# A two-block transformer step: the second block's linear-attention stage put in another order

## Chip, cores and metric

One core of a Trainium2 chip runs the kernel. The metric is device time in microseconds for one execution, lower is better. TensorE (PE) does the matrix products, VectorE (DVE), ScalarE (ACT) and GpSimd (POOL) the element work, SyncE (SP) issues the loads.

## What is computed

256 tokens of width 1024 go through two blocks. The first (windowed attention, latent attention, a large expert lookup) ends with a norm and isn't touched. The second projects the normed tokens to linear-attention queries, keys, values and gates, and to queries, keys and values of a banded attention; both outputs go through one output projection, then a gated feed-forward follows. Cut to what the change touches:

```python
qkv = silu(causal_depthwise_conv(concat([gq, gk, gv]), conv_w))    # 12 tiles of 128 features
q_g, k_g = l2_norm(heads(gq)), l2_norm(heads(gk));  v_g = heads(gv)
beta = sigmoid(gb);  g = -exp(a_log) * softplus(ga + dt_bias)
# per head and chunk of 64 tokens:
G = cumsum(g);  decay = exp(G[:, None] - G[None, :]) where causal
A = (k * beta) @ k.T * decay, strictly lower
u, w = solve(A + I, [v * beta, k * beta * exp(G)])                 # the inverse
qk = q @ k.T * decay, causal
# over the four chunks in turn:
v_new = u - w @ S;  o = (q * exp(G)) @ S + qk @ v_new
S = S * exp(G[-1]) + (k * exp(G[-1] - G)).T @ v_new
o_g = rms_norm(o) * silu(heads(gz))
o_s = sliding_window_attention(rms_norm(sq), rms_norm(sk), sv, sinks)
x = x + gate1 * (concat([o_g, o_s]) @ w_out)
```

## The kernel before

Everything is in `tile_kernel`. A tile framework schedules it: the order in the program text is a priority, an instruction that is ready may go ahead of one that isn't, and each engine then runs its list in the fixed order so found. `issue_after` holds an instruction behind another on its engine.

Large products are made in three passes of reduced-width operands: `Split` (L95, L96) cuts a weight tile into a high part (ScalarE) and a low part (VectorE, or GpSimd for a share `share["pool"]` of them), and `mm3` (L115 to L117) or `features` (L123 to L125) issue high times high and the two mixed products. Small products and transposes are plain float32. `ring` says how many raw and split buffers the weights rotate through.

PSUM has eight banks: four tagged `acc` (`ps_acc`), two `mm` (`ps_mm`), two `tr` (`ps_tr`). The 256 tokens are two blocks b of 128, each of two chunks of 64.

The second block's middle runs as follows. `conv(n)`, n = 0 to 11, makes 128 features of queries (0 to 3), keys (4 to 7) or values (8 to 11): 24 products of 256 columns, two copies on ScalarE, three multiply-adds on VectorE (L1021), a silu (L1022) into `F`. Keys go first; `to_tokens` transposes them, `head_rstd` takes their norm (a power on GpSimd, L142), `kn` is the normed key and `kF` its transpose. Values, then queries follow. Then the decays (L1080 to L1126): cumulated gates, their exponentials `eG`, `eK`, `dec`, `DT`, products with `beta` (`bDT`, `first1`), and on GpSimd `gt`, `bt`, `kbe`, `kd` and `zs`.

`inverse(b, pool)` is a generator: it inverts the triangular matrix in five doubling factors n = 2 to 32, each of a transpose of T (L1186), a copy by ScalarE (L1188), products with A (L1192), a masked copy by VectorE (L1195), products with the transpose (L1199), and a subtraction (L1203). It ends with `wT` and `u`. `recur(b)` walks the two chunks of a block with state `Sb`. `heads` norms the banded attention's queries and keys, `window` makes its scores, softmax (exponentials L1340, division on GpSimd L1347), transposes and product with the values (L1361). `window_heads` is the first half of the output projection, for the banded attention's output `oT`; it needs both blocks.

What order they are in is written at the end: block 0's inverse starts within the query projection `project(0, 512, prq)`, then goes on beside `heads`; block 1's runs beside block 0's recurrence and the rest of `heads` and `window`; block 1's recurrence runs beside `window_heads`. The core lines:

```python
aside = chain(heads(), window())
first = inverse(0, b2)
for k, _ in enumerate(project(0, 512, prq)):
    if k in (3, 6):
        next(first)
...
together(first, (next(aside, None) for _ in range(ASTEPS)))
r0 = recur(0)
together(inverse(1, dr), r0, aside)
...
together(chain(r0, recur(1)), window_heads())
```

`together` takes one step of each generator in turn.

Of the kernel before, what the change touches and what calls it, by code (L numbers as in the profile page):

```python
# [10 lines left out]
F32 = mybir.dt.float32  # L11
# [12 lines left out]
D = 1024  # L24
# [5 lines left out]
def tile_kernel(ctx: ExitStack, tc: tile.TileContext, a, out):  # L30
# [939 lines left out]
    with tc.tile_pool(name="b2", bufs=1) as b2:  # L970
# [4 lines left out]
        for b in range(2):  # L975
            nc.vector.tensor_scalar(x[:, b], x[:, b], rx[:, b, 1:2], math.sqrt(D), op0=OP.mult, op1=OP.mult)
# [32 lines left out]

        F = b2.tile([128, 12, S], F32, name="F")  # L1010

        def conv(n):
            ps = ps_mm([128, S])
            features(ps, weights(a["w_in_f_2"][n]), hh, hl)
# [28 lines left out]
        for n in range(4, 8):  # L1043
            silu = conv(n)
        kps = []
        for b in range(2):
            ps = to_tokens(4, b)
            kps.append((ps, head_rstd(ps, 1.0)))
        kns = []
        for n in range(8, 12):  # L1050
            conv(n)
            if n - KN in (0, 1):
                b = n - KN
                ps, r = kps[b]
                kn = b2.tile([128, 8, 64], F32, tag="kn", name="kn", bufs=2)
                kns.append(kn)
                with tc.issue_after(share["sub"]):
                    nc.vector.tensor_tensor(kn, ps.rearrange("p (h d) -> p h d", h=8), r[:, :8, None].to_broadcast([128, 8, 64]),
                                            op=OP.mult)
        for b in range(2):  # L1060
            ps = ps_tr()
            knf = kns[b].rearrange("p h d -> p (h d)")
            for j in range(4):
                nc.tensor.transpose(ps[:, j * 128:(j + 1) * 128], knf[:, j * 128:(j + 1) * 128], ident)
            nc.scalar.activation(kF[:, :, b * 128:(b + 1) * 128], ps.rearrange("p (j t) -> p j t", j=4), AF.Copy)
        for b in range(2):
            ps = to_tokens(8, b)
            nc.vector.tensor_tensor(vb[:, b], ps.rearrange("p (h d) -> p h d", h=8),
                                    beta[:, b, :, None].to_broadcast([128, 8, 64]), op=OP.mult)
        for n in range(4):  # L1070
            conv(n)
        for b in range(2):
            r = head_rstd(to_tokens(0, b), 1.0)
            nc.vector.tensor_scalar(rq[:, b], r[:, :8], 0.125, None, op0=OP.mult)
        for b in range(2):
            with tc.issue_after(silu.ins):
                zsilu = nc.scalar.activation(zs[:, b].rearrange("p h d -> p (h d)"), prz[b], AF.Silu)


        ps = ps_tr([128, 64])  # L1080
        for b in range(2):
            nc.tensor.matmul(ps[:, b * 8:b * 8 + 8], up, gd[:, b], start=True, stop=True)
        for b in range(2):
            nc.tensor.matmul(ps[:, 16 + b * 8:24 + b * 8], chunk1, gd[:, b], start=True, stop=True)
        for n in range(4):
            nc.tensor.matmul(ps[:, 32 + n * 8:40 + n * 8], chunk1[:, n % 2 * 64:n % 2 * 64 + 1].to_broadcast([128, 128]),
                             gd[:, n // 2], start=True, stop=True)
        p3 = ps.rearrange("p (n h) -> p n h", h=8)
        nc.vector.tensor_copy(Gc, p3[:, 0:2])
        nc.vector.tensor_sub(eK, p3[:, 2:4], Gc)  # L1090
        with tc.issue_after(zsilu.ins):
            nc.scalar.activation(eG, Gc, AF.Exp)
            nc.scalar.activation(eK, eK, AF.Exp)
            nc.scalar.activation(dec, p3[:, 4:8], AF.Exp)


        DT = b2.tile([128, 2, 8, 64], F32, name="DT")
        bDT = b2.tile([128, 2, 8, 64], F32, name="bDT")
        first1 = b2.tile([128, 2, 8, 32], F32, name="first1")
        nG = small.tile([128, 2, 8], F32, tag="nG", name="nG", bufs=1)  # L1100
        nc.vector.tensor_scalar(nG, Gc, -1.0, None, op0=OP.mult)
        sb = small.tile([128, 2, 8], F32, tag="sb", name="sb", bufs=1)
        with tc.issue_after(zsilu.ins):
            nc.scalar.activation(sb, gd, AF.Exp)
        nc.vector.tensor_tensor(sb, sb, beta, op=OP.mult)

        def spread8(t, n):
            return t[:, None].to_broadcast([128, 8, n])

        for b in range(2):  # L1110
# [454 lines left out]
```

## Time and profile before

| what | value |
|---|---|
| three runs, us | 1423.14, 1427.11, 1429.61 (median 1427.11) |
| profiled execution, us | 1425.19 |
| its span, us | 1423.4 |
| mean granted TensorE clock | 0.968 |
| busy: PE, DVE, ACT, POOL | 93%, 77%, 52%, 25% |
| loads from memory | 256.65 MB, 181 GB/s over the span |

The span is the time from the first to the last instruction of the profiled execution. Clock 1.00 is 2.4 GHz, 0.50 is 1.2 GHz. The stage that the change touches lies between 1045 and 1226 us. `1045.33` is the first product of the first convolution, `1114.99` the end of the query projection, `1208.85` the first transpose for the second half of the output projection, and `1225.61` the first transposes of the next norm for block 1.

### The profile page before, as it was taken

What the parts mean: (1) busy time and instruction counts of PE and PEld (TensorE: products, weight loads), DVE (VectorE), ACT (ScalarE), POOL (GpSimd) and SP (SyncE); (2) the same over time, 40 slices, a digit from 0 to 9 for tenths busy, and PEclk for the clock granted to TensorE, in tenths of its full rate; (3) what the DMA queues carried; (4) which work ended last, traced back from release to release, by engine and by line L of the source; (5) the groups of instructions that cost most, each with busy time, mean ns of one, the idle gap of its engine ahead of it and who ended that gap; (6) DMA issues with size and microseconds to landing.
All of it is one profiled execution on the core that took longest, in us unless ns stands there. A gap on an engine that the chain in (4) does not pass through costs nothing.

```text
span 1423.4 us, 25768 instructions
## 1 busy us (share of the span) xinstructions
PE 1326.3 (93%) x9356; PEld 1153.3 (81%) x9356; DVE 1090.6 (77%) x2323; ACT 737.0 (52%) x1562; POOL 354.1 (25%) x291
## 2 busy tenths in 40 slices
PE   5798699999999999999999999999998899899998
PEld 5545589998899999998777778887787667799997
DVE  7788786889788999987777777788778566755555
ACT  3447455555555555456555555555567234555553
POOL 2314332575733333335010010110123120000000
PEclk9799889999999999999999999999999689999999
DMA  9732254554544544458777778788344102455552
GB/s 352 280 124 104 104 163 164 186 168 151 176 151 157 170 164 163 149 167 278 264 243 265 265 256 290 266 307 290 97 141 130 46 2 90 136 191 183 188 188 79
DMA packets 79391, 259.38 MB, mean 182 GB/s; under 512 B 11680, under 2 KB 15776, under 8 KB 79264
## 3 DMA queue, kind: packets, MB, share of 16 engines
q1 hardware_dynamic: 79264, 257.74, 53.4%
q8 instruction: 73, 1.20, 0.3%
q14 instruction: 54, 0.44, 0.1%
HBM read 256.65 MB, written 1.05 MB: 181 GB/s over the span
## 4 chain that ended last, share of the span: by engine, by line
PE 63%; DVE 15%; DMA 9%; issue 6%; POOL 4%; ACT 2%; DVEq 0%; POOLq 0%; ACTq 0%; SPq 0%
PE ps_mm L123 11%; PE ps_mm L125 11%; PE ps_mm L124 11%; DMA raw<-in_w_ada_dram 7%; PE ps_acc L117 6%; PE ps_acc L115 6%; PE ps_acc L116 6%; DVE lo L96 4%; DVE raw L185 3%; PE ps_tr L730 2%; DMA raw<-in_expert_v_dram 1%; POOL W L662 1%; POOL lo L96 1%; POOL rstd L142 1%; ACT hi L95 1%
## 5 line engine op out<-in xcount | busy, mean ns | idle before, releaser
L95 ACT ACTIVATE hi<-raw 128x512 fp32r<-128x512 f32 (+3 forms) x772 | 473.4, 623 | 396.8 <-PE ps_mm L124 192.3
L96 DVE TENSOR_TENSOR lo<-raw,hi 128x512 fp32r<-128x512 f32 (+2 forms) x614 | 452.4, 748 | 147.0 <-ACT hi L95 143.3
L125 PE MATMUL ps_mm<-hh,lo 128*128 128x256 f32 x1600 | 450.9, 282 | 8.5 <-POOL lo L96 5.7
L123 PE MATMUL ps_mm<-hh,hi 128*128 128x256 f32 x1600 | 454.2, 284 | 2.2 <-DVE hh L235 1.9
L124 PE MATMUL ps_mm<-hl,hi 128*128 128x256 f32 x1600 | 449.8, 281 | 0.0
L96 POOL TENSOR_TENSOR lo<-raw,hi 128x512 fp32r<-128x512 f32 (+1 forms) x158 | 226.9, 1437 | 599.9 <-ACT hi L95 556.2
L125 PEld LDWEIGHTS ps_mm<-hh,lo 128*128 128x128 f32 x1600 | 302.1, 189 | 12.0 <-POOL lo L96 7.2
L123 PEld LDWEIGHTS ps_mm<-hh,hi 128*128 128x128 f32 x1600 | 302.0, 189 | 3.9 <-DVE hh L235 2.5
L124 PEld LDWEIGHTS ps_mm<-hl,hi 128*128 128x128 f32 x1600 | 302.2, 189 | 1.2
L117 PE MATMUL ps_acc<-hi,xl 128*128 128x512 f32 x512 | 202.1, 395 | 10.0 <-DVE xl L846 9.8
L116 PE MATMUL ps_acc<-lo,xh 128*128 128x512 f32 x512 | 201.2, 393 | 1.0 <-POOL lo L96 0.6
L115 PE MATMUL ps_acc<-hi,xh 128*128 128x512 f32 x512 | 200.6, 392 | 0.0
L185 DVE SCALAR_TENSOR_TENSOR raw<-raw,cact 128x1024 f32<-128x1024 f32 x86 | 112.0, 1305 | 51.7 <-DMA raw<-in_w_ada_dram 51.2
L117 PEld LDWEIGHTS ps_acc<-hi,xl 128*128 128x128 f32 x512 | 96.5, 188 | 36.1 <-DVE xl L846 16.1
L116 PEld LDWEIGHTS ps_acc<-lo,xh 128*128 128x128 f32 x512 | 96.4, 188 | 24.6 <-DVE lo L96 2.0
L115 PEld LDWEIGHTS ps_acc<-hi,xh 128*128 128x128 f32 x512 | 96.6, 189 | 19.9
L845 ACT ACTIVATE xh<-W 128x256 fp32r<-128x256 f32 x128 | 52.0, 410 | 37.8 <-PE ps_acc L116 35.0
L846 DVE TENSOR_TENSOR xl<-W,xh 128x256 fp32r<-128x256 f32 x128 | 63.6, 499 | 7.6 <-ACT xh L845 7.5
L115 PE MATMUL ps_acc<-hi,sh 128*128 128x512 f32 x120 | 47.8, 400 | 0.3 <-ACT sh L1399 0.3
L117 PE MATMUL ps_acc<-hi,sl 128*128 128x512 f32 x120 | 47.3, 395 | 0.1
L116 PE MATMUL ps_acc<-lo,sh 128*128 128x512 f32 x120 | 47.2, 393 | 0.0
L739 ACT ACTIVATE W<-ps_tr 128x64 f32<-128x64 f32 (+26 forms) x78 | 20.6, 290 | 47.6 <-DVE W L735 36.5
(398 smaller groups left out, 1696.8 us busy)
## 6 DMA issues: line engine op xcount, KB each, us to landing
raw<-in_expert_u_dram SPq DMA_DIRECT2D x128, 512.0 KB, 3.3
raw<-in_expert_v_dram SPq DMA_DIRECT2D x128, 512.0 KB, 4.4
raw<-in_w_ada_dram SPq DMA_DIRECT2D x96, 512.0 KB, 4.7
raw<-in_w_gate_dram SPq DMA_DIRECT2D x22, 512.0 KB, 3.3
raw<-in_w_up_dram SPq DMA_DIRECT2D x22, 512.0 KB, 3.2
raw<-in_w_down_dram SPq DMA_DIRECT2D x22, 512.0 KB, 3.3
raw<-in_w_out_dram SPq DMA_DIRECT2D x16, 512.0 KB, 3.8
raw<-in_w_query_dram SPq DMA_DIRECT2D x16, 512.0 KB, 3.3
```

Of the source, the lines that this page charges most:

```text
L95: nc.scalar.activation(hi[:, :n], raw[:, c0:c1], AF.Copy)
L96: sub = eng.tensor_sub(lo[:, :n], raw[:, c0:c1], hi[:, :n].bitcast(F32))
L115: nc.tensor.matmul(ps, xh, wh, start=start, stop=False)
L116: nc.tensor.matmul(ps, xh, wl, start=False, stop=False)
L117: nc.tensor.matmul(ps, xl, wh, start=False, stop=stop)
L123: nc.tensor.matmul(ps, wh, hh[:, k], start=k == 0, stop=False)
L124: nc.tensor.matmul(ps, wh, hl[:, k], start=False, stop=False)
L125: nc.tensor.matmul(ps, wl, hh[:, k], start=False, stop=k == KT - 1)
L185: nc.vector.scalar_tensor_tensor(w, w, 1.0, act, op0=OP.mult, op1=OP.mult, accum_out=acc)
L730: nc.tensor.matmul(ps[:, i], o2[:, q + i], o[:, q + i], start=n == 0, stop=n == 1)
L845: nc.scalar.activation(xh, W[:, c], AF.Copy)
L846: nc.vector.tensor_sub(xl, W[:, c], xh.bitcast(F32))
```

## The change

The same work is issued in another order.

- The decays become a generator `decay()`, stepped within the convolutions of the keys (n = 4 to 7). Their two GpSimd products per block share one double-width tile, and the silu of the gate `zs` comes right behind the exponentials. The silus of the convolutions are issued later, by `silus()`.
- `conv(n)` is a generator with a step at half its products.
- The normed keys `kn` are made behind the convolutions 8 and 9 (before: 10 and 11), without `issue_after`; `kbe`, `kd` and the gate's product follow the keys' transposes.
- `inverse(b)` of both blocks are stepped together, one step of each per half convolution for n = 10, 11, 0, 1, 2, 3, then one per eighth of the query projection. The products of queries and keys go to the end of `inverse`. T's transposes take `ps_tr` in place of `ps_acc`; all tiles come from pool b2 (A and T four `long` tiles, seven `mat`).
- `heads`, `window` and `window_heads` are one chain, three of its steps per step of `recur(0)`, `recur(1)`. TAIL is 2 instead of 6.
- The scaling of x moves from ahead of the convolutions to behind the query projection; two extra raw and four extra split buffers (pool `dr`) serve the output weights; the tail's normed rows `xn` lie in `F`.

```diff
@@ -972,8 +972,6 @@
         share["pool"] = TSHARE
-        for b in range(2):
-            nc.vector.tensor_scalar(x[:, b], x[:, b], rx[:, b, 1:2], math.sqrt(D), op0=OP.mult, op1=OP.mult)
...
+        def decay():
...
+            nc.scalar.activation(dec, p3[:, 4:8], AF.Exp)
+            nc.scalar.activation(sb, gd, AF.Exp)
+            nc.scalar.activation(eG, Gc, AF.Exp)
+            nc.scalar.activation(eK, eK, AF.Exp)
...
+                gt = b2.tile([128, 4, S], F32, tag="sc", name="gt", bufs=2).rearrange("p h k -> p (h k)")
+                gt = gt.rearrange("p (s h t) -> p s h t", s=2, h=8)
...
+            yield
+            for b in range(2):
+                ps = ps_tr([128, 8, 64])
+                nc.tensor.matmul(ps, chunk1, gts[b][:, 0], start=True, stop=False)
+                nc.tensor.matmul(ps, identb, spread8(past, 64), start=False, stop=True)
+                for h in range(8):
+                    e = nc.scalar.activation(DT[:, b, h], ps[:, h], AF.Exp, bias=nG[:, b, h:h + 1], scale=-1.0)
+                yield e
+            for b in range(2):
+                ps = ps_tr([128, 8, 64])
+                nc.tensor.matmul(ps, chunk1, gts[b][:, 1], start=True, stop=True)
+                nc.vector.tensor_tensor(bDT[:, b], ps, DT[:, b], op=OP.mult)
...
+                if k == KT // 2 - 1:
+                    yield
...
-            return nc.scalar.activation(F[:, n], cy, AF.Silu)
+            made.append((n, cy))
+            yield
+
+        made = []
+
+        def silus():
+            while made:
+                n, cy = made.pop(0)
+                nc.scalar.activation(F[:, n], cy, AF.Silu)
...
-                pt = ps_acc()
+                pt = ps_tr()
...
+        de = decay()
+        for n in range(4, 8):
+            for half, _ in enumerate(conv(n)):
+                if (n, half) in ((4, 1), (5, 0), (5, 1), (6, 0)):
+                    last = next(de)
+                if (n, half) == (5, 1):
+                    for b in range(2):
+                        with tc.issue_after(last.ins):
+                            nc.scalar.activation(zs[:, b].rearrange("p h d -> p (h d)"), prz[b], AF.Silu)
+            if n > 4:
+                silus()
...
+        invs = [inverse(b) for b in range(2)]
+
+        def step():
+            for g in invs:
+                next(g, None)
+
+        for n in (10, 11, 0, 1, 2, 3):
+            for _ in conv(n):
+                step()
+            silus()
...
+        prq = [ps_mm(), ps_mm()]
+        for k, _ in enumerate(project(0, 512, prq)):
+            if k == 1:
+                for b in range(2):
+                    r = head_rstd(to_tokens(0, b), 1.0)
+                    nc.vector.tensor_scalar(rq[:, b], r[:, :8], 0.125, None, op0=OP.mult)
+            step()
...
+        ring((strm, 3, 4), (dr, 2, 4))
+        share["pool"] = 0.0
...
+        aside = chain(heads(), window(), window_heads())
...
+        together(*invs, several(aside, ASTEPS), chain(recur(0), recur(1)))
...
+        xn = F.rearrange("p (b j) t -> p b (j t)", b=3)[:, ::-2]
...
-TAIL = 6
-KN = 10
+TAIL = 2
...
-ASTEPS = 16
+ASTEPS = 3
```

## Rows read from the trace of the kernel before

**Rows 1.** Stages: length; busy PE, PEld, DVE, ACT, POOL; clock, DMA share, GB/s.

```profile
1045.33:1086.50 41.17, 38.94 (x313) 37.27 (x312) 37.39 (x85) 32.56 (x69) 13.82 (x12) 1.00 0.41 129
1086.50:1114.99 28.49, 23.64 (x150) 15.74 (x149) 17.72 (x37) 13.05 (x36) 10.95 (x9) 0.88 0.33 104
1114.99:1208.85 93.86, 84.85 (x1231) 65.60 (x1230) 56.81 (x147) 33.22 (x82) 14.17 (x9) 0.84 0.13 43
1208.85:1225.61 16.76, 12.96 (x59) 9.94 (x58) 11.70 (x22) 6.87 (x16) 1.11 (x2) 1.00 0.29 95
```

**Rows 2.** TensorE's waits, 1045 to 1226: total us, times, longest.

```profile
PE ps_tr L1122 <- DVE bDT L1123: 3.8, 1, 3.8
```

**Rows 3.** Busy time and clock of three stretches.

```profile
1104.00:1111.00 7.00, 5.86 (x13) 4.00 (x14) 4.37 (x10) 0.63 (x1) 1.37 (x2) 0.53 0.23 75
...
1120.00:1145.00 25.00, 22.93 (x369) 18.90 (x371) 11.33 (x42) 8.22 (x25) 3.99 (x3) 0.52 0.01 2
1145.00:1168.00 23.00, 21.16 (x327) 16.51 (x316) 18.59 (x43) 7.89 (x24) 3.74 (x2) 1.00 0.01 1
```

**Rows 4.** TensorE's timeline: start us, us, instruction.

```profile
1045.33 0.28 PE L123 MATMUL ps_mm<-hh,hi 128*128 128x256 f32 x1
...
1053.85 0.28 PE L125 MATMUL ps_mm<-hh,lo 128*128 128x256 f32 x1
...
1095.18 1.13 PE L1116 MATMUL ps_tr<-gt,chunk 128*128 128x512 f32 x2
...
1111.21 0.40 PE L115 MATMUL ps_mm<-hi,hh 128*128 128x512 f32 x1
...
1112.38 0.40 PE L117 MATMUL ps_mm<-hi,hl 128*128 128x512 f32 x1
...
1176.26 0.66 PE L1186 MATMUL ps_acc<-ident,T 128*128 128x128 f32 x4
1176.85 0.67 PE L1192 MATMUL ps_acc<-T,AT 64*64 64x32 f32 x32
1177.44 1.07 PE L1361 MATMUL ps_mm<-PT,kv 128*64 128x512 f32 x2
...
1183.87 1.23 PE L1209 MATMUL ps_acc<-id,T 64*64 64x64 f32 x32 [0.38 <-DVE T L1203]
```

**Rows 5.** By stretches, instructions of tile ps_acc alone (PE, PEld, DVE, ACT).

```profile
1114.99:1148.24 33.25, 18.31 (x436) 15.26 (x434) 6.91 (x23) 4.19 (x8) 0.64 0.06 23
1148.24:1188.70 40.46, 16.87 (x500) 13.81 (x500) 7.72 (x28) 4.22 (x8) 0.92 0.01 2
```

**Rows 6.** Timelines of VectorE and GpSimd near 1048 us.

```profile
1047.57 0.69 DVE L96 TENSOR_TENSOR lo<-raw,hi 128x512 fp32r<-128x512 f32 x1 [0.36 <-ACT hi L95]
...
1049.72 1.54 DVE L96 TENSOR_TENSOR lo<-raw,hi 128x512 fp32r<-128x512 f32 x1
...
1049.67 1.04 POOL L1113 TENSOR_TENSOR gt<-up,ngd 128x512 f32<-128x512 f32 x1 [2.88 <-DVE ngd L1002]
```

**Rows 7.** Chain that ends last: start us, us, what.

```profile
1124.25 1.19 PE ps_mm L1323 x4
...
1177.51 1.00 PE ps_mm L1361 x2
...
1188.75 1.23 PE ps_tr L1246 x8
...
1196.19 1.02 PE ps_tr L1246 x8
```

**Rows 8.** Groups of lines and shapes, 1120 to 1180: busy us, mean ns.

```profile
L1328 DVE SCALAR_TENSOR_TENSOR sc<-dist,ps_mm 128x256 f32<-128x256 f32 x8 | 3.0, 417 | 2.5 <-PE ps_mm L1323 2.5
...
L1333 DVE TENSOR_REDUCE mneg<-sc 128x4 f32<-128x1024 f32 x2 | 2.4, 1210 | 0.0
...
L1340 ACT ACTIVATE sc<-sc,mneg 128x256 f32<-128x256 f32 x8 | 3.9, 494 | 0.3 <-DVE mneg L1336 0.3
...
L1347 POOL TENSOR_TENSOR sc<-sc,sums 128x1024 f32<-128x1024 f32 x2 | 3.7, 1892 | 20.1 <-DVE sums L1345 20.1
```

More of the change, by code (lines that the diff above doesn't have):

```diff
@@ L1041, in head_rstd @@
             return rstd_of(ss, 8, scale)
[L1043 to L1094, printed above, removed]
@@ new lines, in tile_kernel @@
+        kps = []
+        for b in range(2):
+            ps = to_tokens(4, b)
+            kps.append((ps, head_rstd(ps, 1.0)))
+        kns = []
+        for n in (8, 9):
+            for _ in conv(n):
+                pass
+            silus()
+            b = n - 8
+            ps, r = kps[b]
+            kn = b2.tile([128, 8, 64], F32, tag="kn", name="kn", bufs=2)
+            kns.append(kn)
+            nc.vector.tensor_tensor(kn, ps.rearrange("p (h d) -> p h d", h=8), r[:, :8, None].to_broadcast([128, 8, 64]),
+                                    op=OP.mult)
@@ new lines, in tile_kernel @@
+        for b in range(2):
+            ps = ps_tr()
+            knf = kns[b].rearrange("p h d -> p (h d)")
+            for j in range(4):
+                nc.tensor.transpose(ps[:, j * 128:(j + 1) * 128], knf[:, j * 128:(j + 1) * 128], ident)
+            nc.scalar.activation(kF[:, :, b * 128:(b + 1) * 128], ps.rearrange("p (j t) -> p j t", j=4), AF.Copy)
+            be = small.tile([128, 8], F32, tag="be", name="be", bufs=2)
+            nc.vector.tensor_tensor(be, beta[:, b], eG[:, b], op=OP.mult)
+            nc.gpsimd.tensor_tensor(kbe[:, b], kns[b], be[:, :, None].to_broadcast([128, 8, 64]), op=OP.mult)
+            nc.gpsimd.tensor_tensor(kd[:, b], kns[b], eK[:, b, :, None].to_broadcast([128, 8, 64]), op=OP.mult)
+            nc.gpsimd.tensor_tensor(zs[:, b], zs[:, b], gdnw[:, None, :].to_broadcast([128, 8, 64]), op=OP.mult)
@@ new lines, in tile_kernel @@
+        invs = [inverse(b) for b in range(2)]
[3 more added lines that the diff above has]
+        for n in (10, 11, 0, 1, 2, 3):
+            for _ in conv(n):
+                step()
+            silus()
+            if n == 11:
+                for b in range(2):
+                    ps = to_tokens(8, b)
+                    nc.vector.tensor_tensor(vb[:, b], ps.rearrange("p (h d) -> p h d", h=8),
+                                            beta[:, b, :, None].to_broadcast([128, 8, 64]), op=OP.mult)
@@ new lines, in tile_kernel, with several @@
+        pw = [[ps_acc(), ps_acc()], [ps_acc(), ps_acc()]]
+        aside = chain(heads(), window(), window_heads())
+        def several(g, n):
+            while True:
+                for _ in range(n):
+                    if next(g, g) is g:
+                        return
+                yield
+        together(*invs, several(aside, ASTEPS), chain(recur(0), recur(1)))
+        dr.release()
+        at.release()
+        ff = tc.alloc_tile_pool(name="ff", bufs=1, side="right")
+        ring((strm, 3, 4), (ff, 2, 4))
@@ new lines, in tile_kernel, with residual @@
+        xn = F.rearrange("p (b j) t -> p b (j t)", b=3)[:, ::-2]
+        g_rows = [F[:, i * 4 + 4:i * 4 + 8].rearrange("p j t -> p (j t)") for i in range(2)]
+        g_row = row_of(mod[:, 16:24], None, None, g_rows[0])
+        def residual(pw, g_row, b, n):
+            cs = slice(n * 512, (n + 1) * 512)
+            tt = b2.tile([128, 512], F32, tag="PT", name="tt", bufs=2)
+            nc.vector.tensor_tensor(tt, pw[b][n], g_row[:, cs], op=OP.mult)
+            nc.vector.tensor_add(x[:, b, cs], x[:, b, cs], tt)
```

131 lines of the change are left out of this document (54 added, 77 removed).

## Prediction

> **What bounds the kernel now.** I read the page's busy times and slices first, to find where in the span the change lies, then that part by stages, then who waits in it, the clock, the chain that ends last, and single instructions. TensorE is the busiest engine in every stage [rows 1], so what isn't TensorE work is mostly hidden, and what can be won is time in which TensorE idles or is slow. The change lies in 1045 to 1226 us, cut here into the convolutions (41.17 us), decays and query projection (28.49), both inverses with attention, recurrence and first half of the output projection (93.86), and a tail (16.76) [rows 1]. The first is dense: TensorE busy 38.94 of 41.17 at full clock. The second is not: 23.64 of 28.49 at 0.88. The third is busy on paper, 84.85 of 93.86, but at a mean clock of 0.84. So a reader who looks only at busy shares misses the loss. The list of waits names its start: 3.8 us before the second product of the decays, for the vector engine [rows 2]. The clock rows show what follows: 0.53 for the next 7 us though dense products run, and 0.52 for 25 us from 1120, while block 0's inverse, the heads and block 0's softmax run, against 1.00 from 1145 to 1168 with scores, recurrence and inverse mixed [rows 3]. Half clock here is 1.2 GHz, 1.00 is 2.4 GHz.
>
> **What moves.** The work stays the same but for its order: no product, copy or load of any size is removed. So the sum is made of two stretches: the first up to the end of the query projection (69.66 us before, the first two lines of [rows 1]), which takes in the decays earlier and both inverses; and the second up to the last half of the output projection (93.86), which loses the inverses. The tail I leave at 16.76: its products wait for the same residual and norm steps; the normed rows' new place in F is free once the recurrence has read it.
>
> **First stretch, TensorE at full clock.** The 72 products of three convolutions start from 1045.33 to 1053.85, 0.120 us apart [rows 4]; 288 make 34.6. The projection's 48 go at 0.234 (five steps from 1111.21 to 1112.38): 11.2. A transpose of 128 columns takes 0.59/4 = 0.15 by the distance from 1176.26 to 1176.85; 32 make 4.7. Decays: per block two products like the one of 1.13 and a bf16 one of a quarter of it, 4.8 for both blocks less a drain; their sixteen 8-column products at no more than a transpose, 1.8 (an estimate): 6.6. An inverse has five factors of four transposes (0.59), 32 products (0.59, from 1176.85 to 1177.44) and 32 more, taken alike: 8.9; three sets of 32 with 64 columns at 1.23 [rows 4]: 3.7; the two products of the keys together 1.4, between 1.2 and 2.5 by the same rows. That is 14.0. Two rows bear it out: block 1's inverse keeps TensorE 16.87 us at 0.92, which is 15.5; block 0's 18.31 at 0.64 is 11.7, and a part of it fell before this row begins [rows 5]. Two inverses: 28. In all 34.6 + 11.2 + 4.7 + 6.6 + 28 = 85.1 us.
>
> How full will it be? A chain of one factor waits twice for the vector engine and once for ScalarE; alone it left holes. Beside it now lie two half convolutions per turn and the other block, so the nearest row is the convolutions' own: 34.6 + 24 transposes at 0.15 = 38.2 of 41.17, 93%. 85.1/0.93 = 91.5. Bounds: no hole at all, 85.1; the filling of the whole first stretch of before, (34.6 + 11.2 + 4.7 + 6.6 + 1.4)/69.66 = 84%, 101.3. Cover for the other engines: the vector engine was busy 37.39 + 17.72 = 55.1 there and takes on 6.91 + 7.72 = 14.6 of the inverses [rows 1, 5], 70 of 91.5; ScalarE 45.6 and some 9, far from full. The deferred silus cost nothing: their input waits in one of eight buffers, ScalarE has room, and the PSUM banks are freed by the two copies ahead of them. The gate's silus wait on ScalarE for the last exponential of DT, as they waited for a silu before; queued behind them are the next convolution's two copies, and TensorE waits for these only when both banks are full. If this cover goes, TensorE waits for a bank; that is in the upper bound. The gain of the removed 3.8 us wait, and of the slow 7 us behind it, is in this sum already, since it is made at full clock. The stretch grows by 21.8 (15.4 to 31.6).
>
> **The one cost that speaks against it: GpSimd beside the vector engine.** The products gt, first, kbe, kd and zs on GpSimd now all run while the vector engine is needed by convolutions. A low part of the weights takes it 0.69 at 1047.57 and 1.54 at 1049.72, beside a GpSimd product of 1.04 [rows 6]: 0.85 lost in 1.04, 82%. GpSimd was busy 10.95 in the second stage [rows 1]; if all of it fell on the vector engine's path, 9.0 us. I take none of this beyond the 93%, because the convolution stretch had 13.82 of GpSimd already, and it is the second rival's price. The Trainium skill (SBUF — State Buffer, Who interferes with whom) says that an instruction with two SBUF inputs on VectorE and one of GpSimd that reads SBUF exclude each other for the whole instruction. By it the price would be up to 10.95 rather than 9.0; the trace agrees in kind, with 82% in place of all.
>
> **Second stretch.** What ends last is now one chain: heads, softmax of block 0, softmax of block 1, then the first half of the output projection, which needs both blocks. Before, it went from the projection's end at 1114.99 to the first scores at 1124.25 and to the end of the last product with the values at 1178.5 [rows 7]: 9.3 and 54.3. The heads keep their 9.3: two sums, two powers on GpSimd, nothing of the inverse in their way. Block 1's own steps are 1.2 + 3.0 (scores), 2.4 + 0.6 (maxima), 3.9 (exponentials), 0.9, 3.7 (GpSimd) [rows 8] (0.6 and 0.9 are estimates) and 5.6 for transposes and the product with the values, whose eight halves take 0.5 each (1.07 for two with their drain, [rows 4]): 21.3. Block 0 has half the columns: 11 to 21, near 15. So the two softmaxes take between 32.3, their own steps, and the 54.3 of before. I take 41: nearer to the lower end, for the inverse that filled the gap (18.31 and 16.87 of TensorE, 14.6 of the vector engine) is gone and the recurrence alone lies beside. Copy and split to the first output product: three steps of at most 0.60, 1.4. Then 48 products at 0.234, 11.2, no longer behind the second recurrence. In all 9.3 + 41 + 1.4 + 11.2 = 62.9; from 9.3 + 32.3 + 1.2 + 11.2 = 54 to 9.3 + 54.3 + 1.8 + 11.2 + 3.3 = 79.9, the last 3.3 being what 7 us at a clock of 0.53 lose [rows 3]. The recurrence is shorter than this chain: before, a chunk began 7.4 us after the one ahead of it [rows 7], so four take some 30. Its vector work queues against the softmax; that is the way from 15 + 21.3 to 41. The scaling of x, moved here, is two instructions of 1024 columns, below 1.21 each by the maxima's row [rows 8], hidden since nothing needs x before the tail. The loads of the output weights go on SP's queue behind the projection's, with two more slots; DMA was 0.13 busy here [rows 1], so they land before ScalarE and the vector engine split them, early and off the chain. The stretch loses 31.0 (14.0 to 39.9).
>
> **Sum.** 91.5 + 62.9 = 154.4 against 163.5: 9.1 us less. The profiled execution took 1425.19 (span 1423.4), giving 1416.1; the three runs' median is 1427.11, 1.9 above it, giving 1418.0. I say 1417. One measurement of this kernel tells about 0.5% (7 us) from no change.
>
> **Rivals.** *All hidden* (15%): both softmaxes run near their own steps and the filling reaches 95%: 89.6 + 56 = 145.6, 18 us less, 1408. For it: 1.00 from 1145 to 1168. Against: the vector engine was busy 18.59 of 23 there [rows 3]. *The first stretch gives it back* (22%): GpSimd's 9.0 falls on the inverses' chain, the filling stays at 84%: 101.3 + 62.9, 0.7 us more, 1427; between, part of it. For it: vector rows of 0.69 that became 1.54; against: the other block fills. *The clock stays low* (18%), which ends on the other side: without the inverse TensorE has too little to do from the heads to the second softmax, as from 1120. Then the softmaxes take their old 54.3 and 4.0 more for block 1's eight halves, the output projection 14.5: 9.3 + 58.3 + 1.4 + 14.5 = 83.5, 11.5 us more, 1437. It is a loss once the second stretch passes 72, and slower by over 0.5% from 79. Against it: the recurrence is dense in small products, and the same mix stood at 1.00 for 23 us.
>
> **Numbers.** My forecast has 45%, from 3 to 15 us less. Faster by over 0.5%: three quarters of it, and the first rival, 50%. Same: 11% of the forecast, half of the second rival and a little of the third, 26%. Slower: the rest of these two, 24%. The range from 1403 to 1437 takes in the first rival and the third's middle; the forecast's own is 1410 to 1424.
>
> **What would show it.** Right: end of the query projection about 92 us after the first convolution's product, clock 1.00 until there, no wait of the decays' products above 1 us; then some 63 us to the output weights' second half, with recurrence done before block 1's copy. Wrong: vector engine above 95% in the first stretch with lows of 1.5 us; a granted clock of 0.5 between the heads and the output projection; or the last inverse steps still running after the projection.

## The result: 1.06% slower, and the profile after

| | before | after |
|---|---|---|
| median, us (4 runs each) | 1426.06 (1423.14 to 1429.61) | 1439.80 (1438.91 to 1446.66) |
| ratio | | 1.0106, 95% interval 1.0066 to 1.0145 |
| span of the profiled execution, us | 1423.4 | 1436.9 |

The forecast was 1417 with a range up to 1437; the time is 13.7 us above before's and outside the range.

The stages of the profiled execution after, to be read against the first two, the third and the fourth line of [rows 1]. First comes the stretch from the first convolution's product to the end of the query projection, then the one up to the first transposes for the output projection's second half, then the tail:

```profile
1042.38:1143.25 100.87, 92.25 (x1395) 79.95 (x1393) 67.92 (x172) 53.37 (x119) 26.02 (x22) 0.92 0.24 75
1143.25:1222.56 79.31, 51.27 (x294) 38.67 (x294) 40.85 (x94) 25.76 (x67) 13.26 (x8) 0.78 0.13 46
1222.56:1239.11 16.55, 12.79 (x59) 10.01 (x59) 12.61 (x23) 8.18 (x18) 1.11 (x2) 1.00 0.45 156
```

The first stretch grew by 31.2 us (69.66 to 100.87; forecast 21.8), the second shrank by 14.6 (93.86 to 79.31; forecast 31.0). The tail stayed. Look at TensorE's busy column. The second stretch lost 33.6 us of TensorE work (84.85 to 51.27) and only 14.6 us of time: its idle time went from 9.0 us to 28.0. That is the row that explains most of the result, as the experiments show. The first stretch, at a mean granted clock of 0.92, missed its forecast for a reason of its own, told below.

Single windows of after, same columns: the decays beside the convolutions, both inverses beside convolutions and projection, then three windows in the softmaxes.

```profile
1053.00:1062.00 9.00, 8.60 (x55) 6.69 (x53) 4.18 (x12) 8.93 (x24) 0.08 (x1) 1.00 0.00 1
1094.00:1126.00 32.00, 32.00 (x738) 29.02 (x730) 22.10 (x66) 15.64 (x33) 0.95 (x1) 1.00 0.27 75
1162.00:1170.00 8.00, 0.01 (x2) 0.01 (x1) 3.22 (x9) 3.39 (x17) 1.10 (x2) 0.66 0.00 1
1170.00:1179.00 9.00, 9.00 (x38) 6.05 (x38) 2.97 (x6) 1.61 (x3) 0.94 (x1) 0.55 0.00 0
1179.00:1194.00 15.00, 3.40 (x15) 1.57 (x14) 7.95 (x19) 4.95 (x19) 3.11 (x2) 0.70 0.00 0
```

With the inverses beside the convolutions TensorE has no hole for 32 us at full clock. In the softmaxes it does nothing for 8 us and then runs at a granted clock of 0.55, where before stood at 1.00 with the second inverse beside it (the window from 1145 in [rows 3]). TensorE's two longest waits in the second stretch (total us, times, longest):

```profile
PE ps_tr L1330 <- POOL sc L1321: 18.5, 2, 10.5
PE ps_tr L1278 <- DVE q L1270: 6.9, 2, 6.6
```

L1330 are the transposes of the scaled scores. TensorE's timeline shows what else stood in its list, from the first scores (L1297) to the last product with the values (L1335) and the first of the output projection (L115):

```profile
1154.75 0.71 PE L1297 MATMUL ps_mm<-kT,qT 64*128 64x128 f32 x4
...
1160.97 1.04 PE L1229 MATMUL ps_tr<-Sb,F 128*64 128x128 f32 x8
1170.00 1.11 PE L1330 MATMUL ps_tr<-ident,sc 128*128 128x128 f32 x4 [7.99 <-POOL sc L1321]
1171.04 2.07 PE L1235 MATMUL ps_tr<-vn,kd 64*128 64x128 f32 x8
1173.04 1.96 PE L1244 MATMUL ps_tr<-vn,DT 64*64 64x64 f32 x16
1174.94 1.97 PE L1335 MATMUL ps_mm<-PT,kv 128*64 128x512 f32 x2
...
1194.47 1.12 PE L1330 MATMUL ps_tr<-ident,sc 128*128 128x128 f32 x4 [10.49 <-POOL sc L1321]
1195.52 1.97 PE L1220 MATMUL ps_tr<-Sb,wT 128*64 128x128 f32 x8
1197.28 1.70 PE L1229 MATMUL ps_tr<-Sb,F 128*64 128x128 f32 x8
...
1204.88 1.08 PE L1335 MATMUL ps_mm<-PT,kv 128*64 128x512 f32 x4
...
1207.64 0.50 PE L115 MATMUL ps_acc<-hi,sh 128*128 128x512 f32 x1
```

Recurrence products (L1220 to L1244) stand behind the waiting transposes in the fixed list, so they don't use the wait, and after it they run ahead of the softmax's next product. My first theory was built on these lines; it fell.

### The profile page after: what moved, and what is told of

Read it like the earlier page. It is cut to its first block, busy times and chain, and to the rows that moved or that the text cites. A ratio compares the mean times of both kernels' runs of the same rounds, so it can differ in the third digit from the quotient of the medians.

```text
span 1436.9 us, 25758 instructions
## 1 busy us (share of the span) xinstructions
PE 1321.1 (92%) x9356; PEld 1151.9 (80%) x9356; DVE 1089.3 (76%) x2323; ACT 739.1 (51%) x1563; POOL 353.8 (25%) x291
## 4 chain that ended last, share of the span: by engine, by line
PE 62%; DVE 14%; DMA 11%; issue 5%; ACT 4%; POOL 3%; DVEq 0%; SPq 0%; POOLq 0%; ACTq 0%
PE ps_mm L123 11%; PE ps_mm L125 11%; PE ps_mm L124 11%; DMA raw<-in_w_ada_dram 8%; PE ps_acc L115 6%; PE ps_acc L117 6%; PE ps_acc L116 6%; DVE lo L96 4%; DVE raw L185 2%; PE ps_tr L730 2%; DMA raw<-in_expert_v_dram 2%; ACT hi L95 1%; POOL W L662 1%; POOL rstd L142 1%; DVE xl L846 1%
## 5 line engine op out<-in xcount | busy, mean ns | idle before, releaser
L95 ACT ACTIVATE hi<-raw 128x512 fp32r<-128x512 f32 (+3 forms) x772 | 473.3, 623 | 406.4 <-PE ps_mm L124 193.4
L125 PE MATMUL ps_mm<-hh,lo 128*128 128x256 f32 x1504 | 423.4, 282 | 7.9 <-POOL lo L96 5.7
L123 PE MATMUL ps_mm<-hh,hi 128*128 128x256 f32 x1504 | 427.1, 284 | 1.9 <-DVE hh L235 1.9
L124 PE MATMUL ps_mm<-hl,hi 128*128 128x256 f32 x1504 | 422.5, 281 | 0.0
L125 PEld LDWEIGHTS ps_mm<-hh,lo 128*128 128x128 f32 x1504 | 283.9, 189 | 11.1 <-POOL lo L96 7.2
L123 PEld LDWEIGHTS ps_mm<-hh,hi 128*128 128x128 f32 x1504 | 283.9, 189 | 3.3 <-DVE hh L235 2.5
L124 PEld LDWEIGHTS ps_mm<-hl,hi 128*128 128x128 f32 x1504 | 283.7, 189 | 1.4 <-DVE hl L236 0.2
L115 PE MATMUL ps_acc<-hi,xh 128*128 128x512 f32 x512 | 200.2, 391 | 0.0
L115 PEld LDWEIGHTS ps_acc<-hi,xh 128*128 128x128 f32 x512 | 96.1, 188 | 20.2 <-ACT hi L95 0.4
L115 PE MATMUL ps_acc<-hi,sh 128*128 128x512 f32 x120 | 47.5, 398 | 0.3 <-ACT sh L1341 0.3
```

The costliest lines, as they stand in the source:

```text
L95: nc.scalar.activation(hi[:, :n], raw[:, c0:c1], AF.Copy)
L115: nc.tensor.matmul(ps, xh, wh, start=start, stop=False)
L123: nc.tensor.matmul(ps, wh, hh[:, k], start=k == 0, stop=False)
L124: nc.tensor.matmul(ps, wh, hl[:, k], start=False, stop=False)
L125: nc.tensor.matmul(ps, wl, hh[:, k], start=False, stop=k == KT - 1)
```

## Experiments

In the table, ratios are to the kernel before, timed beside it. The columns behind them are from each profiled execution: the first stretch; the rest, from the projection's end to the first transposes of the next norm (those of block 0); and both together, the block.

| kernel | ratio (95%) | first | rest | block |
|---|---|---|---|---|
| before | 1 | 69.66 | 106.83 | 176.49 |
| after | 1.0106 (1.0066 to 1.0145) | 100.87 | 92.07 | 192.94 |
| e1 recurrence alone | 1.0203 (1.0172 to 1.0234) | 98.46 | 106.98 | 205.44 |
| e5 recurrence in projection | 1.0156 (1.0120 to 1.0192) | 113.05 | 83.64 | 196.69 |
| e2 one step of attention | 1.0095 (1.0060 to 1.0131) | 98.41 | 90.75 | 189.16 |
| e6 scaling on VectorE | 1.0089 (1.0051 to 1.0127) | 96.87 | 93.93 | 190.80 |
| e3 silus behind decays | 1.0112 (1.0087 to 1.0138) | 95.45 | 95.23 | 190.68 |
| e4 GpSimd products late | 1.0107 (1.0074 to 1.0139) | 100.37 | 95.64 | 196.01 |
| e7 inverse 1 beside attention | 1.0050 (1.0017 to 1.0082) | 84.58 | 94.73 | 179.31 |
| e8 the same and silus | 1.0025 (1.0002 to 1.0048) | 81.92 | 95.30 | 177.22 |
| e9 fillers in e1 | 1.0220 (1.0174 to 1.0265) | 98.35 | 104.51 | 202.86 |
| e10 decays alone | 1.0031 (1.0008 to 1.0054) | 74.03 | 104.78 | 178.81 |
| e11 try for best | 1.0048 (1.0024 to 1.0072) | 81.83 | 101.49 | 183.32 |
| e12 decays alone and silus | 1.0017 (0.9998 to 1.0037) | 73.75 | 106.40 | 180.15 |

One execution tells stretches to some 4 us: the first stretch, in which after, e1, e2, e6 and e9 have one and the same order, took 96.9 to 100.9 us. The second stretch of after, e3 and e4, in which all engines have the same order, took 79.3, 82.5 and 82.9 us. A difference of a few us in one profile is not a finding by itself.

**Is it the recurrence's place in TensorE's list? e1, e5, e2.** e1 puts all of it ahead of the heads:

```diff
-        together(*invs, several(aside, ASTEPS), chain(recur(0), recur(1)))
+        together(*invs)
+        for _ in chain(recur(0), recur(1)):
+            pass
+        together(aside)
```

> The changed kernel with the whole recurrence ahead of the heads, nothing of it beside the banded attention, so that the softmaxes and the copies of the split have TensorE to themselves. In the changed kernel the stretch from the end of the query projection to the first transpose of the gated output is 79.3 us, of which heads and softmaxes take 62.7 and the out-projection of the window's heads and the copy before it 15. Theory A (TensorE's fixed list: recurrence products stand behind transposes that wait for GpSimd's scaling, then stand in front of the softmax's next products): the chain from the heads' first square to the last copy of the window falls from 62.7 to 50 to 53 us with nothing in its way, the wait for GpSimd's scaled scores (18.5 us in the changed kernel) to about 12, the last piece of the recurrence no longer lies in the out-projection; the recurrence alone costs some 24 to 28 us ahead, so that the stretch is 88 to 94 and the kernel some 10 slower than the changed one. Rival B (heads and softmaxes are as long by themselves, by their own waits and TensorE's low clock): that chain stays at 60 us or more, the stretch is 98 to 104, the kernel 20 or more slower.

The kernel is slower than after by some 14 us (ratios 1.0203 and 1.0106). The window in e1 from the recurrence's end to the end of the last transposes ahead of the output projection (columns as above), and TensorE's timeline in it: the last piece of the recurrence, the heads' first transposes, the first scores, the last product with the values.

```profile
1166.91:1222.25 55.34, 24.42 (x86) 14.48 (x86) 18.18 (x51) 16.77 (x49) 11.30 (x7) 0.57 0.00 1
```

```profile
1165.77 1.14 PE L1244 MATMUL ps_tr<-vn,DT 64*64 64x64 f32 x16
1176.10 1.09 PE L1278 MATMUL ps_tr<-ident,q 128*128 128x128 f32 x4 [9.19 <-DVE q L1270]
...
1180.12 0.77 PE L1297 MATMUL ps_mm<-kT,qT 64*128 64x128 f32 x2 [2.73 <-DVE kT L1282]
...
1219.41 1.82 PE L1335 MATMUL ps_mm<-PT,kv 128*64 128x512 f32 x4
```

With nothing beside them the two softmaxes take 41.1 us (1180.12 to 1221.23), in after 51.2 (1154.75 to 1205.96). So the recurrence does cost them 10 us, but it costs 26.8 by itself ahead of them (1140.09 to 1166.91). The heads take 13.2 from its end to the first scores, not 9.3. Heads and softmaxes together, 54.3 (62.7 in after), are between what A and B expected.

e5 starts the recurrence in the projection:

```diff
+        rec = chain(recur(0), recur(1))
         for k, _ in enumerate(project(0, 512, prq)):
...
-            step()
+            if k < 3:
+                step()
+            else:
+                next(rec, None)
```

> The changed kernel with the recurrence's first five pieces (of eight) stepped through the query projection's last five rows of weights, where its predecessor stepped nothing; the other three pieces stay beside the banded attention. Theory A (the recurrence queued in TensorE's fixed list is what makes the second stretch long): the projection grows by the pieces' own products, some 8 us (about 64 products of at most 0.1 to 0.2 us each), filled and at full clock, and the stretch behind it falls from 79.3 to 60 to 66 us: the kernel is 6 to 12 us faster than the changed one, 1428 to 1434. Rival B (the softmaxes by themselves are the length): the stretch stays at 74 or more and the projection grows: no gain or a loss of some us.

Four pieces moved, not five (the fifth step is one of the empty ones that TAIL adds). The first stretch grew by 12.2 and the rest shrank by 8.4; the kernel is slower than after, if by anything, not 6 to 12 us faster. Theory A's gain isn't there.

e2 sets ASTEPS to 1, so that the list holds all four chunks before the first scaled score's transposes:

> The changed kernel with one step of the attention to one of the recurrence, not three. TensorE's list then has all four chunks of the recurrence ahead of the first transposes of scaled scores, between the heads' transposes and the first scores; none stands behind a wait for GpSimd and none in the out-projection. Theory A (the recurrence queued behind the waits is what makes the second stretch long): it falls from 79.3 to 66 to 72 and the kernel is 6 to 12 us faster than the changed one. Theory E (there is too little work beside the softmaxes whatever its order, and what is put in the heads' gaps delays the first scores by as much): it stays at 76 to 84, the kernel within 5 us of the changed one.

The order came out as meant, the output projection then runs without recurrence, and still the time is after's. TensorE still waits for the scaled scores, now with nothing left to stand behind:

```profile
PE ps_tr L1330 <- POOL sc L1321: 15.5, 4, 10.3
```

Theory A falls: no other place of the recurrence made the kernel faster than after. That there is too little to fill this stretch, theory E, is so far argued only; e7 tests it.

**Is it GpSimd's scaling? e6** (`nc.gpsimd` to `nc.vector` in the softmax's last step):

> The changed kernel with the four scalings of the softmaxes' scores on VectorE in place of GpSimd (1.04 and 1.89 us each there); TensorE's list is the same. In the changed kernel TensorE waits 18.5 us for them in two waits, behind reductions, exponentials and sums. If the scaling itself is what is waited for, the waits fall by 3 us and more, and the second stretch from 79.3 to 74 to 76; by theory E the waits fall by no more than the difference of the durations, some 2 us in all, and the kernel is within 3 us of the changed one: the wait is the softmax's whole chain on VectorE and ScalarE.

```profile
PE ps_tr L1330 <- DVE sc L1321: 16.7, 2, 9.1
```

The wait fell by 1.8 us; the second stretch (81.2) and the time did not. What TensorE waits for is the row of maxima, exponentials, sums and scaling, not the engine at its end.

**Is it the low clock? e9** adds to e1 idle products behind each softmax's scores:

```diff
+                with tc.issue_after(last.ins):
+                    for _ in range(FILL[b]):
+                        nc.tensor.matmul(pw[0][0], identb, spread8(past, 64), start=True, stop=True)
```

> The kernel with the recurrence alone ahead of heads and softmaxes, and idle products (18 and 30 of 128x512, bfloat16, into a bank that the out-projection overwrites later) put behind each softmax's score products, so that TensorE runs while GpSimd and ScalarE work; they compute nothing that is used. Without them the chain from the end of the recurrence to the last product of the window is 56.0 us at a granted clock of 0.57. Theory G (the low clock is a good part of the chain's length, since every transpose and product on it takes twice as long): the clock in that stretch rises over 0.8 and the chain falls to 47 to 52. Rival H (the chain is VectorE, ScalarE and GpSimd, and the clock is not what sets it): the chain stays within 2 us of 56.

The same window in e9, from the recurrence's end:

```profile
1170.05:1222.82 52.77, 33.93 (x134) 17.80 (x134) 18.36 (x51) 16.66 (x49) 11.29 (x7) 0.74 0.00 1
```

The mean clock rose from 0.57 to 0.74 and the window shrank by 2.6 us (55.3 to 52.8; the expected text's 56.0 counts from 0.7 us before the recurrence's end), which one profile hardly tells from nothing; the timed ratio (1.022 against 1.0203) shows no gain. In this stretch the clock is not the main cost, though at 0.74 it isn't fully tried.

**Is it the decays' place? e3, e4.** In after's decays ScalarE is busy 8.93 of 9 us (first window above). Its timeline there:

```profile
1052.77 1.75 ACT L1051 ACTIVATE DT<-ps_tr,nG 128x64 f32<-128x64 f32 x8 [0.80 <-PE ps_tr L1049]
...
1055.18 1.28 ACT L1090 ACT_TABLE_LOAD   x1
1056.47 0.42 ACT L1090 ACTIVATE F<-cy 128x256 f32<-128x256 f32 x1
1056.89 1.28 ACT L1051 ACT_TABLE_LOAD   x1
1058.19 1.75 ACT L1051 ACTIVATE DT<-ps_tr,nG 128x64 f32<-128x64 f32 x8
1059.95 1.28 ACT L1364 ACT_TABLE_LOAD   x1
1061.25 1.08 ACT L1364 ACTIVATE zs<-ps_acc 128x512 f32<-128x512 f32 x2
...
1063.15 1.17 ACT L95 ACTIVATE hi<-raw 128x512 fp32r<-128x512 f32 x2
```

A deferred silu (L1090) fell between the two blocks' exponentials; with it come two more table loads of 1.28 us, and the high parts of the weights (L95) that the convolutions need come behind all of it. The Trainium skill (ScalarE: Activation LUTs, What ACT_TABLE_LOAD costs) counts a drain of about 1.38 us on top of each load; the trace shows none here, the silu starts 0.01 us after its load has ended, so a switch costs 1.28. e3 holds these silus back:

```diff
-            if n > 4:
+            if n == 5:
+                with tc.issue_after(last.ins):
+                    silus()
+            elif n > 5:
                 silus()
```

> The changed kernel with the silus of the fourth and fifth feature blocks held behind the last of the decays' 16 exponentials, so that ScalarE has no silu between them. Theory C (ScalarE is full for 12 us in the decays and delays the high parts of the weights; each change between exponential and silu loads a table, 1.28 us): two loads fewer, TensorE's waits for high parts and for the silu at 1062 to 1067 (together 3.1 us in the changed kernel) go, and with them the low clock at 1067 to 1073: the first stretch falls from 100.9 to 94 to 98, the kernel is 3 to 7 us faster than the changed one. Rival D (the loss of the first stretch is at the keys, where VectorE and GpSimd share the lock): at most 1 us.

The first stretch is 95.5, against 96.9 to 100.9 in the five kernels with after's order; e8 against e7 says the same, 81.9 against 84.6; e12 against e10 nothing. Most of this is the granted clock: the time in which TensorE does nothing fell by 1 us only, from 8.6 to 8.9 in those five kernels to 7.7 in e3, and from e7 to e8 by 0.2, while the mean clock there rose from 0.96 to 0.98. The timed kernel didn't move. So theory C is worth 3 us at most, and in the changed kernel not measurable.

e4 moves six GpSimd products (four of the keys, two of the gate) behind the first products of the inverses:

```diff
+                i = nc.gpsimd.tensor_tensor(kbe[:, b], kns[b], be[:, :, None].to_broadcast([128, 8, 64]), op=OP.mult)
+                with tc.issue_after(i.ins):
+                    nc.gpsimd.tensor_tensor(kd[:, b], kns[b], eK[:, b, :, None].to_broadcast([128, 8, 64]), op=OP.mult)
...
+            if n == 10:
+                late()
```

> The changed kernel with the six GpSimd products of the keys (keys times decays, the gate's weight) issued behind the first product that both inverses wait for, not before it. Theory D (the first rows of the inverses wait 2.9 us on VectorE because its copies and GpSimd's products slow each other, and the clock then stays low for 10 us): the wait at the first transposes of the inverses falls under 1 us, the first stretch from 100.9 to 95 to 98, the kernel is 3 to 6 us faster than the changed one. Rival C (ScalarE's queue in the decays is the loss): at most 1 us, and the wait only moves to the keys times values.

TensorE's waits there in e4:

```profile
PE ps_tr L1101 <- ACT F L1090: 2.9, 2, 1.8
...
PE ps_tr L1156 <- DVE T L1147: 0.3, 1, 0.3
```

The wait for T went from 2.9 us to 0.3, as theory D says, and the one for a silu rose from 1.1 to 2.9. One wait took most of the other's place: TensorE's idle time in the stretch fell by 0.8 us, from 8.6 to 7.8. The granted clock was no higher, 0.91 in the mean, and the stretch stayed at 100.4. So theory D is right on the wait and wrong on what it is worth.

**Is it the filling that was taken away? e7, e8, e10.** e7 puts only the second inverse back beside the attention:

```diff
-            for g in invs:
-                next(g, None)
+            next(invs[0], None)
...
-        together(*invs, several(aside, ASTEPS), chain(recur(0), recur(1)))
+        together(*invs, recur(0), several(aside, ASTEPS))
+        pw = [[ps_acc(), ps_acc()], [ps_acc(), ps_acc()]]
+        together(recur(1), window_heads())
```

with ASTEPS 2. e8 is e7 with e3's edit. e10 has inverses, recurrence and attention in the order of before, so that of the change the decays' move and the small edits around it are left (silus, normed keys, scaling of x, banks and pools).

> The changed kernel with the second token block's inverse taken out of the projections and put back beside the heads and softmaxes, with the first block's recurrence; the second block's recurrence lies beside the out-projection of the window's heads, two steps of the attention to one of the inverse. Between the first convolution's product and the end of the block the kernel before has 160.4 us of TensorE busy in 180.3, the changed one 156.3 in 196.7: idle 19.9 against 40.4, of which the second stretch has 9.0 against 28.0. Theory E (the change took the inverses, the work that filled TensorE beside the softmaxes, and put them where TensorE was the bound): the first stretch falls by the inverse's own TensorE work at full clock, about 14 us (100.9 to 86 to 88), the second takes it into its idle time and stays at 74 to 82; the kernel is 8 to 14 us faster than the changed one, 1426 to 1432, and TensorE's idle in the second stretch falls from 28 to under 15. Rival F (whatever stands beside the softmaxes is queued in their way, the recurrence or an inverse): the second stretch grows by what the first loses, to 88 or more, and the time stays within 4 us of the changed kernel's.

> The kernel of the run with the second inverse beside the attention, and the silus of the fourth and fifth feature blocks held behind the last of the decays' exponentials. In the changed kernel that order alone shortened the first stretch from 100.9 to 95.5 us but not the time. Theory C (ScalarE's queue in the decays holds up the high parts): another 3 to 5 us off the first stretch, and off the time, since the second stretch now has filling; 1422 to 1428. Rival: the gain is given back in the second stretch again, no difference to the run without it.

> Of the change only the decays' move beside the first four convolutions (with the later silus and the values' transposes as in the changed kernel); both inverses, the recurrence and the attention stand as in the kernel before. Theory E: the first stretch, freed of both inverses (28 us of TensorE work), is 70 to 75 us, the second is as before, 90 to 94: the decays' move gains about what it costs, and the kernel is 1422 to 1432, within 6 us of before. Rival C (the decays' place is where the change loses: ScalarE's queue beside the convolutions): first stretch 78 or more, the kernel at 1433 or more.

The two stretches of e7 (cut as in after, the second up to the output projection's second half):

```profile
1044.42:1129.00 84.58, 76.08 (x899) 65.12 (x900) 60.95 (x142) 49.29 (x111) 26.86 (x22) 0.96 0.28 88
1129.00:1211.01 82.01, 69.42 (x795) 53.03 (x795) 50.15 (x125) 29.43 (x75) 13.71 (x8) 0.81 0.13 46
```

The pair that shows the second inverse's place with the narrower intervals is e3 and e8. It is not a clean one: in e8 the second recurrence, which needs that inverse, lies beside the output projection, and two steps of the attention go with one of the inverse. e3:

```profile
1050.46:1145.91 95.45, 87.75 (x1395) 76.29 (x1393) 68.21 (x172) 50.65 (x117) 27.00 (x22) 0.95 0.25 80
1145.91:1228.42 82.51, 54.18 (x294) 39.45 (x295) 40.89 (x94) 25.76 (x67) 13.80 (x8) 0.75 0.13 45
```

e8:

```profile
1043.49:1125.41 81.92, 73.60 (x899) 63.79 (x900) 60.20 (x142) 46.36 (x109) 27.14 (x22) 0.98 0.29 92
1125.41:1207.98 82.57, 70.57 (x795) 54.60 (x795) 50.57 (x125) 29.60 (x75) 13.73 (x8) 0.79 0.13 46
```

In the second stretch TensorE has 16.4 us more work (54.18 to 70.57), and the stretch is 0.1 us longer; beside the projections the inverse costs 13.5. The time follows: 1.0112 falls to 1.0025, with intervals that don't touch. The 0.1 us is a balance: heads and softmaxes took 5.2 us less (65.9 to 60.7), as the inverse came and half of the recurrence left, and the output projection's stage 5.3 more (16.6 to 21.9), where that half went. No run moves this half alone; e1, e2 and e5 moved the recurrence in other ways and gained nothing, so it isn't a likely source of the gain. In e7 TensorE waits for the scaled scores 1.6 us in all, not 18.5:

```profile
PE ps_tr L1330 <- POOL sc L1321: 1.6, 2, 0.9
```

Theory E holds for the second inverse, and rival F, that an inverse there would be queued in the softmaxes' way, falls. e10's stretches:

```profile
1049.14:1123.17 74.03, 63.74 (x467) 54.42 (x469) 55.80 (x121) 47.27 (x106) 26.82 (x22) 0.95 0.34 108
1123.17:1215.22 92.05, 81.85 (x1227) 65.44 (x1227) 57.45 (x147) 32.20 (x80) 13.58 (x8) 0.85 0.11 36
```

For the first inverse the place was not free: from e10 to e7 the first stretch grew by 10.6 us and the second shrank by 10.0. In e10 TensorE is busy for 81.85 of the second stretch's 92.05 us, so taking 12.4 us of work away shortened it. In e7 it is busy for 69.42 of 82.01; with the second inverse gone as well (after), for 51.27 of 79.31, and the time hardly follows.

From these blocks the change's 16.5 us (192.94 less 176.49) can be split: the decays' move with the small edits 2.3 (e10 less before), the first inverse's 0.5 (e7 less e10), the second's 13.6 (after less e7). By the timed ratios it is 4, 3 and 8 of 15 us, with e7's runs spread from 1422 to 1440; for the second, e3 and e8 give 12 (0.87% of 1424).

**Can a mixture beat both? e11, e12.** e11 is e8 with e4's edit and the attention's steps written first:

```diff
-        together(*invs, recur(0), several(aside, ASTEPS))
+        together(several(aside, ASTEPS), *invs, recur(0))
```

> A try for a kernel that beats both: the second inverse beside the attention, the silus behind the decays' exponentials, the keys' six GpSimd products behind the first product of the inverses, and the attention's steps written ahead of the inverse's in the second stretch, so that inverse and recurrence fill behind it. The run without the last two took 81.9 us in the first stretch and 82.6 in the second. If the order in TensorE's list is what the second stretch loses (GpSimd's scaled scores and the heads first), it falls to 76 to 80 and the kernel to 1416 to 1423, faster than before by up to 0.5%. If TensorE's own work at its mixed clock is the bound (70.6 us busy in 82.6 at 0.79), it stays within 2 us, and the kernel stays where before is, 1423 to 1430.

> Of the change the decays' move alone, now with the silus of the fourth and fifth feature blocks behind the last of the decays' exponentials. The decays' move alone took 74.0 and 92.1 us in the two stretches, 2.3 more than before in all. Theory C (ScalarE's table loads and exponentials hold up the high parts beside the convolutions): the first stretch is 70 to 72 and the kernel the same as before within 0.4%. Rival: the gain of this order is given back behind it, as it was in the changed kernel, and the kernel stays 0.3% slower than before.

Neither does. In e11 the inverse's first factor now waits for VectorE, behind the attention's work there:

```profile
PE ps_tr L1330 <- POOL sc L1321: 6.3, 3, 4.4
PE ps_acc L1162 <- DVE T L1147: 5.0, 1, 5.0
```

e12, the decays' move with e3's edit, takes the time of before within 0.4%. No kernel here is faster than before.

## Why the prediction was wrong

**The second stretch, from 54.3 to 41 for the softmaxes: this step failed.** I argued that "the inverse that filled the gap ... is gone and the recurrence alone lies beside", and read the inverse as what had made 54.3 of it. It had not. 41.1 is right for softmaxes with nothing beside them (e1). With the recurrence they take 51.2 in after, and 54.4 and 54.3 in e3 and e4, whose engines have the same order there; in before, with the inverses too, 54.3. The lines of e3, first scores and last product with the values:

```profile
1157.45 0.71 PE L1297 MATMUL ps_mm<-kT,qT 64*128 64x128 f32 x4
...
1210.75 1.08 PE L1335 MATMUL ps_mm<-PT,kv 128*64 128x512 f32 x4
```

So taking the inverses out from beside them shortened them by 3 us in one execution and not at all in two. What the stretch did lose lay behind the softmaxes. In before the output projection started 12.3 us after the last product with the values (1178.5), behind the second inverse's end and the recurrence's next products; in after 1.7. Before:

```profile
1190.78 0.51 PE L115 MATMUL ps_acc<-hi,sh 128*128 128x512 f32 x1
```

The sum had this gain, and credited 13.3 us of the softmaxes on top of it. The other terms were too small as well: heads 11.5 for 9.3, copy and split 1.7 for 1.4, output projection with the recurrence's last pieces in it 14.9 for 11.2. Together 79.3 for 62.9.

**The first stretch, 91.5 for 100.9: the full clock failed.** The sum is made for "TensorE at full clock", 85.1 us. TensorE was busy for 92.25 at a mean clock of 0.92, which is some 85 at full clock (an estimate): the work was right, and its density nearly, 8.6 us without TensorE work where 85.1 in 91.5 leaves 6.4. So of the missing 9.4 us the lower clock took 7.2, and idle time 2.2. Nearly all the idle time, 8.3 us, lies ahead of 1094. In the decays ScalarE was not "far from full" but busy for 8.93 of 9 us, and TensorE's waits behind it come to 3.1 us; at the inverses' start TensorE waited 2.9 us for T. After such waits the granted clock fell (0.55 from 1067 to 1073, 0.66 from 1084 to 1094), but not each time. e6 has the same order and the same wait of 2.9 us for T. The 8 us behind that wait, in after and in e6:

```profile
1086.18:1094.18 8.00, 8.00 (x148) 7.00 (x149) 4.86 (x18) 2.13 (x4) 0.52 (x1) 0.58 0.18 61
```

```profile
1087.59:1095.59 8.00, 8.00 (x199) 7.20 (x199) 6.76 (x23) 3.51 (x8) 1.28 (x1) 1.00 0.22 76
```

I had set 101.3 as the bound; it is where the stretch ended in after, and e6's took 96.9. That "deferred silus cost nothing" was wrong in kind, two table loads, though not measurably in time (e3).

**The rivals.** The second, the first stretch gives it back by GpSimd's work beside the vector engine, was right in size only; e4 took away one such wait and gained nothing. Its price of 82% rests on one row, and the next GpSimd product, from 1050.67 us, lay beside that subtraction too and took 1.49 us, not 1.04, so each engine held up the other. The third rival named the stretch that failed and its cause, that TensorE has too little to do from the heads to the second softmax, and gave 1437 at 83.5 us. The clock did stay low there (0.78), but the rival put the price on it, of which e9 recovers 2.6 us at 0.74, where most of the loss is the idle time itself. I had weighed it at 18%, against it "the recurrence is dense in small products". The row beside that sentence could have told: the 327 TensorE instructions in those 23 us [rows 3] are the inverse's as well as the recurrence's, and no row had shown the recurrence alone.

**Open:** what the decays' move itself costs (e10 +0.31%, interval 0.08 to 0.54; e12 +0.17%, interval -0.02 to 0.37) is not told apart from nothing with certainty. Why the clock fell behind the wait for T in after and not in e6 no run shows. And no run moves the second recurrence without the second inverse.

## What to carry to other kernels

A chain that waits on other engines can take in work almost for nothing: the second inverse, 16.4 us of TensorE work, cost 0.1 us there and 13.5 beside projections that keep TensorE full. But removing work helps as long as TensorE is the limit: the first inverse's leaving gave back 10.0 of the 10.6 us that it cost elsewhere. So price a move at the place it goes to. Credit the place it leaves only down to the length of the other engines' chain, and have a row that shows this length. Read idle time of the bounding engine per stage before and after a planned move: here 16.5 us of idle in a block of 176.5, and what the low clock cost besides, was all there was to win, and the change made it 37.0 in 192.9. And when several waits lie in a row in one stage, removing the longest alone can gain nothing.

## What the runs showed of the hardware

Executions reach the changed stage at different times, though TensorE's list ahead of it is the same: the first convolution's product starts at 1041.2 to 1050.6 us in the thirteen profiles of changed kernels, at 1045.3 in that of before. They differ by as much at an earlier product, the fiftieth L115 into PSUM tag acc, which starts between 151.05 and 159.18 us in the fourteen profiles. So stretches were compared, not spans.

The granted clock differed between executions of one order. The second stretch, with the same order on all engines, stood at 0.78 in after, 0.75 in e3 and 0.73 in e4, and took 79.3, 82.5 and 82.9 us. In the first stretch the five kernels with one order left TensorE idle for 8.6 to 8.9 us each, and took 96.9 us at a mean clock of 0.96 (e6) to 100.9 at 0.92 (after).
